# Interleaving two tensors on one core: eight equal column tiles, or tiles of 7168, 8320 and 8384 columns

## The chip, the cores and the metric

The kernel runs on one core of one Trainium2 chip. The metric is device time in microseconds for one execution, as a median over runs. The core has several compute engines, of which this kernel uses VectorE (DVE in the profile) for copies, and 16 DMA engines that move data between HBM, the chip's main memory, and SBUF, the core's working memory of 128 partitions. SyncE (SP) and ScalarE (ACT) compute nothing here; each issues transfers into a DMA queue of its own, and the same 16 DMA engines serve both queues.

## What is computed

Two float32 arrays are interleaved element by element along the last dimension.

```python
def setup_inputs():
    batch, seq, dim = 32, 256, 1024
    return {"x": randn(batch, seq, dim), "y": randn(batch, seq, dim)}   # float32

def reference(x, y):
    result = np.zeros((batch, seq, dim * 2), dtype=np.float32)
    result[..., 0::2] = x
    result[..., 1::2] = y
    return result
```

As the last dimension is doubled throughout, the arrays can be taken as flat: element i of x goes to place 2i of the output, element i of y to place 2i+1. Each input has 8,388,608 elements or 33.55 MB; 67.11 MB are read and 67.11 MB written.

## The kernel before

The flat arrays are cut into eight consecutive pieces. Piece number t starts at element `start` and holds 128 x `lw` elements, with `lw` = `WL` = 8192. A piece is read as 128 rows of `lw` consecutive elements, one row for each SBUF partition, so that neighbouring rows lie `lw` x 4 = 32,768 B apart in HBM. The output rows belonging to it are `2 * lw` elements long, 65,536 B apart.

Each piece is handled as follows.

- x and y are loaded whole into `xtile` and `ytile` (lines 58 and 59), 4 MiB each, by transfers issued from SP. Each of the two pools has two buffers, so the loads of piece t+2 wait until the copies of piece t have read the buffer.
- The piece is then worked in halves of `WS` = 4096 columns. For each half VectorE copies the x half into the even columns of `otile` (line 80) and the y half into the odd columns (line 81). `otile` has 8192 columns and two buffers, so the copy of a half waits until the store of the half before the previous one has landed.
- Each filled `otile` is stored by one transfer of 4 MiB issued from ACT (line 82). Its rows are 32,768 B long and 65,536 B apart in HBM.

The first piece differs in two points. Its x is loaded in two column halves, one issued from SP and one from ACT (line 53). After its y has landed, ACT issues a small early store (line 67), 16 rows of 128 elements from `ytile` to the place of the last piece in the output, where the last piece's own stores write the final values later.

Order around the change: SP's queue holds, in order, half of the first x, the first y, then x and y of each later piece. ACT's queue holds the other half of the first x, the early store and then the sixteen stores, numbered 1 to 16 in what follows, two for each piece. VectorE works in program order except that both x copies of the first piece run before its y copies. [...]

After the program is built, `tile_interleave_kernel` moves the first load of SP and of ACT into the opening block and shortens the closing block. The change does not touch this.

Of the kernel before, what the change touches and what calls it, by code (L numbers as in the profile page):

```python
# [3 lines left out]

# [4 lines left out]


@with_exitstack
def _interleave(
    ctx: ExitStack,
    tc: tile.TileContext,
    x: bass.AP,
    y: bass.AP,
    out: bass.AP,
):
    nc = tc.nc  # L20
    P = 128

    total = 1
    for s in x.shape:
        total *= s

    WL = 8192
    WS = 4096

    xf = x.rearrange("b s d -> (b s d)")  # L30
    yf = y.rearrange("b s d -> (b s d)")
    of = out.rearrange("b s d -> (b s d)")

    fp32 = mybir.dt.float32

    xpool = ctx.enter_context(tc.tile_pool(name="xp", bufs=2))
    ypool = ctx.enter_context(tc.tile_pool(name="yp", bufs=2))
    opool = ctx.enter_context(tc.tile_pool(name="op", bufs=2))

    lwidths = [WL] * (total // P // WL)  # L40
    assert sum(lwidths) == total // P

    start = 0
    for lw in lwidths:
        xtile = xpool.tile([P, WL], fp32, name="xtile")[:, :lw]
        ytile = ypool.tile([P, WL], fp32, name="ytile")[:, :lw]

        xs = dataclasses.replace(xf, offset=start, ap=[[lw, P], [1, lw]])
        ys = dataclasses.replace(yf, offset=start, ap=[[lw, P], [1, lw]])
        if start == 0:  # L50

            for q, c in ((nc.sync, 0), (nc.scalar, lw // 2)):
                q.dma_start(
                    out=xtile[:, c : c + lw // 2],
                    in_=dataclasses.replace(xf, offset=c, ap=[[lw, P], [1, lw // 2]]),
                )
        else:
            nc.sync.dma_start(out=xtile, in_=xs)
        nc.sync.dma_start(out=ytile, in_=ys)

        if start == 0:


            early = dataclasses.replace(
                of, offset=2 * (total - P * WL), ap=[[2 * WL, 16], [1, 128]]
            )
            nc.scalar.dma_start(out=early, in_=ytile[:16, :128])

        soff = 0
        while soff < lw:  # L70
            width = min(WS, lw - soff)
            otile = opool.tile([P, 2 * WS], fp32, name="otile")[:, : 2 * width]
            os_ = dataclasses.replace(
                of,
                offset=2 * start + 2 * soff,
                ap=[[2 * lw, P], [1, 2 * width]],
            )
            xsub = xtile[:, soff : soff + width]
            ysub = ytile[:, soff : soff + width]
            nc.vector.tensor_copy(out=otile[:, 0::2], in_=xsub)  # L80
            nc.vector.tensor_copy(out=otile[:, 1::2], in_=ysub)  # L81
            nc.scalar.dma_start(out=os_, in_=otile)
            soff += width

        start += P * lw
    assert start == total


def kernel(tc, x, y, out):
    nc = tc.nc  # L90
    _interleave(tc, x, y, out)
    tc.close()
    tc.compile()  # L93


    blocks = nc.main_func.blocks
    for engine in (mybir.EngineType.SP, mybir.EngineType.Activation):
        opening = blocks[0].instructions
        at, moved = next(
            (b, i)  # L100
            for b in blocks[1:]
            for i in b.instructions
            if i.engine == engine and i.opcode == "DMACopy"
        )
        assert not moved.sync_info.on_wait
        body = at.instructions
        body.remove(moved)
        gate = next(
            n
            for n, i in enumerate(opening)  # L110
            if i.engine == engine and i.opcode == "Drain"
        )
        opening.insert(gate, moved)
        at.instructions = body
        blocks[0].instructions = opening

    last = nc.main_func.blocks[-1]  # L120
    tail = last.instructions
    wait = tail[0]
    clear = next(n for n, i in enumerate(tail) if i.opcode == "ISA")
    assert wait.engine == mybir.EngineType.SP and wait.opcode == "Drain"
    assert wait.sync_info.on_wait and not wait.sync_info.on_update
    assert tail[clear].engine == mybir.EngineType.Pool
    last.instructions = [
        copy.replace(wait, engine=mybir.EngineType.Pool)
    ] + tail[clear:]


# [1 line left out]
_INS = ['x', 'y']  # L133
_OUTS = [((32, 256, 2048), 'float32')]


# [23 lines left out]
```

## Time and profile before

| what | value |
|---|---|
| median of 3 runs | 315.62 us (315.53 to 315.71) |
| profiled execution, its own time | 315.62 us |
| its span, first to last instruction | 313.8 us |
| bytes moved | 134.23 MB in 4784 DMA packets |
| mean rate over the span | 428 GB/s |
| share of 16 DMA engines, ACT's queue (q10) and SP's queue (q1) | 51.1% and 48.4% |
| VectorE copies, 32 of them | 2295 ns (line 80) and 2293 ns (line 81) each |
| median from issue to landing: store, y load, x load | 29.1, 60.8, 43.6 us |

The span is shorter than the time because it holds only what lies between the first and the last instruction on the core. A DMA packet here is one row going to or from one partition, or a small write that signals completion. The 128 rows of a transfer are shared out over 16 DMA engines, eight to each.

The waits of the compute engines, longest first, show what VectorE waits for: the columns are the waiting engine and line, what it waited for, the total in us, how often, and the longest.

```profile
DVE otile L80 <- DMA out_dram<-otile: 174.2, 14, 21.8
DVE otile L81 <- DMA ytile<-in_y_dram: 39.9, 8, 5.8
DVE otile L80 <- DMA xtile<-in_x_dram: 11.7, 1, 11.7
```

Line 80 waits 14 times for a store to free its `otile`; line 81 waits once in each piece for y. Both are waits for DMA transfers.

### The profile page before, as it was taken

The numbers are of one execution on the slowest core, as the hardware profiler recorded it, in microseconds if no ns is written. First come the engines' busy times: TensorE is split into PE (matmuls) and PEld (weight loads), VectorE is DVE, ScalarE is ACT, GpSimd is POOL, SyncE is SP. The second block draws the span as 40 slices with busy tenths as digits, with TensorE's granted clock in tenths as the row PEclk, the third lists the DMA queues.
The fourth block names the chain that finished last, engine by engine and source line by source line (L and its number), as shares of the span: only waits on it lengthen the run. The fifth ranks groups of instructions, "written<-read, shape, count | busy, mean of one in ns | idle before, by whom it ended". The sixth has DMA issues, their size and how long they took to land.

```text
span 313.8 us, 139 instructions
## 1 busy us (share of the span) xinstructions
DVE 72.6 (23%) x32; POOL 0.2 (0%) x4
## 2 busy tenths in 40 slices
DVE  0523002231022410325003150031501305023500
POOL 0000000000000000000000000000000000000000
DMA  8999999999999999999999999999999999999997
GB/s 340 462 405 398 459 409 459 409 459 409 459 409 447 422 439 430 426 443 422 447 414 455 409 459 401 468 401 464 405 464 405 464 405 459 409 459 409 459 409 334
DMA packets 4784, 134.23 MB, mean 428 GB/s; under 512 B 544, under 2 KB 560, under 8 KB 560
## 3 DMA queue, kind: packets, MB, share of 16 engines
q10 hardware_dynamic: 2480, 69.22, 51.1%
q1 hardware_dynamic: 2304, 65.01, 48.4%
HBM read 67.11 MB, written 67.12 MB: 428 GB/s over the span
## 4 chain that ended last, share of the span: by engine, by line
DMA 83%; DVE 11%; DVEq 1%; issue 0%
DMA out_dram<-otile 76%; DMA ytile<-in_y_dram 7%; DVE otile L81 6%; DVE otile L80 5%; DVEq L93 1%; DVEq L80 0%
## 5 line engine op out<-in xcount | busy, mean ns | idle before, releaser
L80 DVE COPY otile<-xtile 128x4096 f32<-128x4096 f32 x16 | 36.6, 2295 | 185.9 <-DMA out_dram<-otile 174.2
L81 DVE COPY otile<-ytile 128x4096 f32<-128x4096 f32 x16 | 36.6, 2293 | 39.9 <-DMA ytile<-in_y_dram 39.9
L144 POOL MEMSET const-bfloat16-1.0<- 128x1 bf16 x1 | 0.1, 101 | 0.0
L144 POOL MEMSET const-uint8-127<- 128x1 uint8 x1 | 0.1, 101 | 0.0
L144 POOL MEMSET const-float32-0.0<- 128x1 f32 x1 | 0.1, 98 | 0.2 <-issue 0.2
L144 POOL MEMSET const-float32-1.0<- 128x1 f32 x1 | 0.1, 98 | 0.0
## 6 DMA issues: line engine op xcount, KB each, us to landing
out_dram<-otile ACTq DMA_DIRECT2D x16, 4096.0 KB, 29.1
ytile<-in_y_dram SPq DMA_DIRECT2D x8, 4096.0 KB, 60.8
xtile<-in_x_dram SPq DMA_DIRECT2D x7, 4096.0 KB, 43.6
xtile<-in_x_dram SPq DMA_DIRECT2D x1, 2048.0 KB, 11.6
xtile<-in_x_dram ACTq DMA_DIRECT2D x1, 2048.0 KB, 13.3
out_dram<-ytile ACTq DMA_DIRECT2D x1, 8.0 KB, 6.2
```

The source lines that it names most:

```text
L80: nc.vector.tensor_copy(out=otile[:, 0::2], in_=xsub)
L81: nc.vector.tensor_copy(out=otile[:, 1::2], in_=ysub)
L93: tc.compile()
L144: nc = _bacc.Bacc("TRN2", target_bir_lowering=False, num_devices=1)
```

## The change

The list of widths becomes one piece of 7168 columns, five of 8320 and two of 8384, which again add up to 65,536 columns. `WL`, now 8384, is the width of the buffers and of the last piece. `WS` is set anew for each piece to half its width, so there are still two halves, two copies for each half and one store for each half: 3584, 4160 or 4192 columns to a half. The rows of the loads are now 28,672, 33,280 or 33,536 B long and as far apart; the stores' rows are as long and twice as far apart.

```diff
-    WL = 8192
-    WS = 4096
+    WL = 8384
...
-    lwidths = [WL] * (total // P // WL)
+    lwidths = [7168] + [8320] * 5 + [8384] * 2
     assert sum(lwidths) == total // P
...
             nc.scalar.dma_start(out=early, in_=ytile[:16, :128])
 
+        WS = lw // 2
         soff = 0
         while soff < lw:
             width = min(WS, lw - soff)
-            otile = opool.tile([P, 2 * WS], fp32, name="otile")[:, : 2 * width]
+            otile = opool.tile([P, WL], fp32, name="otile")[:, : 2 * width]
```

The number of loads, copies and stores, and the bytes that they move, stay the same. The early store's place in the output follows `WL`, as it is worked out from the start of the last piece.

## The prediction

> **What bounds the kernel now.** I read the page's busy shares first, then its DMA rows, then busy time by window, then the timeline and the waits. The page's engine row and its two slice rows:
>
> ```profile
> DVE 72.6 (23%) x32; POOL 0.2 (0%) x4
> ...
> DMA  8999999999999999999999999999999999999997
> GB/s 340 462 405 398 459 409 459 409 459 409 459 409 447 422 439 430 426 443 422 447 414 455 409 459 401 468 401 464 405 464 405 464 405 459 409 459 409 459 409 334
> ```
>
> VectorE is busy for a quarter of the span, the DMA engines for nine tenths or more in all slices but the first and the last. The slices swing between 401 and 468 GB/s only because a packet's bytes are counted where it starts and a slice holds a broken number of packets. Windows cut at one tile's period show no swing; the columns are window, length, VectorE busy (instructions), POOL busy, clock, DMA share, GB/s:
>
> ```profile
> 67.56:106.29 38.73, 9.09 (x4) 0.00 (x0) 1.00 1.00 433
> 106.29:145.01 38.72, 9.09 (x4) 0.00 (x0) 1.00 1.00 433
> 145.01:183.74 38.73, 9.09 (x5) 0.00 (x0) 1.00 1.00 433
> 183.74:222.46 38.72, 9.09 (x4) 0.00 (x0) 1.00 1.00 433
> 222.46:261.19 38.73, 9.09 (x5) 0.00 (x0) 1.00 1.00 433
> ```
>
> Five tiles at five different addresses take the same time to 0.01 us, 16.777 MB in 38.726 us, or 433.2 GB/s. Two more windows separate the directions, loads alone early and stores alone late:
>
> ```profile
> 11.65:22.00 10.35, 4.51 (x3) 0.00 (x0) 1.00 1.01 434
> ...
> 294.00:310.00 16.00, 4.43 (x2) 0.00 (x0) 1.00 1.01 434
> ```
>
> Loads alone, which step by 32 KiB from row to row, stores alone, which step by 64 KiB, and the mixture all run at 433 to 434. [...] The trace's packet records, which lie beneath these views, agree: of 3968 rows of 32 KiB, 3931 last exactly 1213 ns. A slow address would show as a longer row, and the longer ones but for ten are the 27 around 26 to 28 us discussed below. So the kernel is bound by the 16 DMA engines' own pace: 32 rows per engine and tile in 38.726 us, 1.2102 us for a row of 8192 columns.
>
> The time outside that pace: 134.23 MB at 433.2 is 309.85 us, and the span is 313.80, so 3.95 us lie around it. By windows, the first 2 us carry 139 GB/s and lose 1.36, the next two carry 385 and lose 0.22, the stretch from 22 to 48, where stores join the loads, carries 424 and loses 26 x (1 - 424/433.2) = 0.55, and 1.80 after 312 start no packet. Together 3.93. The profiled run took 315.62, which is 1.82 more than its span and equal to the median.
>
> **The change, part by part.** *Bytes and rows.* Eight tiles stay eight tiles, each with 32 rows per engine (8 of x, 8 of y, twice 8 of output). Scaling the row by columns, the new sum per engine is 32 x (1.0589 + 5 x 1.2291 + 2 x 1.2386) = 309.8 us, the old one 32 x 8 x 1.2102 = 309.8. A fixed cost within a row cancels too, as there are 256 rows either way. Term: 0.
>
> *The pitch.* What it can give is bounded below by nothing and above by the fastest window of some length: stores alone from 300 to 306 carry 437 GB/s, and 134.23/0.437 is 2.7 us less than 309.85; but a six-microsecond window holds five packets per engine, so that is mostly counting. In the other direction a pitch that is no power of two could stretch rows; the nearest rows for that are the ten single rows of 1216 to 1226 ns, 13 ns over the usual, and on all 256 rows of an engine that would be +3.3 us. I take 0, because the row time is the same at every address, direction and both present pitches.
>
> [...]
>
> *Copies on VectorE.* 32 copies stay 32, of 3584, 4160 and 4192 columns in place of 4096, at 2294 ns per 4096: about 2.01, 2.33 and 2.35 us. The total stays 72.6. They hide behind transfers in flight; without that cover a tile of 8384 pays 4 x 0.05 = 0.2 us more.
>
> *The start.* The first tile has 1024 columns less, so its y lands 2 x 1024 x 4 x 128 B / 433.2 = 2.42 us earlier than 21.98; its two y copies end with the first store's issue 0.28 sooner still, 24.31 becoming about 21.6. SP's later issues move with it: x of the third tile, now at 16.18, and its y, now at 28.23 behind the small early store. None of this shortens the end, because the load queue holds x and y of the second tile, issued at 1.30 and 1.94, until 55.46: the engines were busy then and still are. What is paid once when stores join, 0.55 us, could disappear or double, depending on where in a row the first store arrives. I take it unchanged; bounds -0.55 and +0.55.
>
> *The end.* The last store may not start late, so its queue must never run dry. The timeline there, with start, length, and in brackets the idle time and what ended it:
>
> ```profile
> 280.64 2.29 DVE L80 COPY otile<-xtile 128x4096 f32<-128x4096 f32 x1 [14.95 <-DMA out_dram<-otile]
> 287.81 2.29 DVE L81 COPY otile<-ytile 128x4096 f32<-128x4096 f32 x1 [4.88 <-DMA ytile<-in_y_dram]
> 290.13 8.67 ACTq L82 DMA_DIRECT2D out_dram<-otile  x2
> 293.93 2.30 DVE L80 COPY otile<-xtile 128x4096 f32<-128x4096 f32 x1 [3.83 <-DMA out_dram<-otile]
> 296.14 2.29 DVE L81 COPY otile<-ytile 128x4096 f32<-128x4096 f32 x1
> ```
>
> The last y lands at 287.81, its copy ends at 290.1, store 15 is issued, and store 14 lands at 293.84. Store 15 took 13.4 us to land, so 303.53, which is 9.69 after store 14: eight rows at 1.21, no gap. By the packet records, store 14's last rows end at 293.05 to 293.58 across engines, and the kernel's first load needed 1.0 to 2.2 us from issue to the first row on an engine. The cover is therefore 1.2 to 1.9 us. Who waits if it is gone: store 15, then the copies at 293.93 (for store 14's buffer), then store 16 behind store 15 on Activation's queue.
>
> How the cover moves depends on how many rows of store 14 are left when loads end; now it is five. The packet records show the two queues taking turns row by row, so this number is set only by how many rows of the second tile's x pass alone before the first store joins: six now, and five or six after, as the store is issued 0.28 us (a quarter of a row) sooner after y. Five left give 0.14 more cover from longer rows less 0.04 for the longer copy. Four left take off 1.24 and leave 0.1 to 0.8. I take no gap; bounds 0 and +1.5, the latter from the rival below. In the steady part the cover is larger: a first-half store is issued near 96.5 and the one before it lands at 106.2.
>
> Sum: 0 + 0 + 0 + 0 + 0; the span stays 313.8, the time 315.6.
>
> **Rivals.** *A gap before the last tile's first store* (slower). If the queues share by bytes rather than rows, the earlier start of the stores (2.42 + 0.28 = 2.7 us) pushes the loads' end back by as much; less the cover of 1.2 to 1.9 that is a gap of 0.8 to 1.5 us, about 316.8. It decides from the point where under four rows of store 14 remain when the last y lands. For it: the 3.71 us between 290.13 and 293.84 are the shortest distance in the trace. Against: the rows' strict alternation. Chance 0.14.
>
> *Rows longer than 32 KiB get cut in two, or otherwise cost a bit more each* (slower). Seven tiles have rows of 33,280 and 33,536 B. The first tile's 16 KiB rows follow one another at 607 ns, so a cut costs 2 x 607 - 1210 = 4 to 5 ns, on 28 transfers of 8 rows per engine 1.0 us: 316.6. For it: no row here is over 32,768 B. Against: nothing at that size shows a limit. Chance 0.07.
>
> *The pitch does cost today, evenly on all rows* (faster). Half of the 2.7 us bound gives 314.3. For it: a uniform loss is invisible in a comparison of rows. Against: 32 KiB loads and 64 KiB stores agree to 1 GB/s. With the switch cost of 0.55 vanishing beside a little of this, chance 0.19.
>
> **How the numbers follow.** No change beyond 0.2% (0.63 us, about what a measurement of this kernel tells from nothing) has 0.60, all of it the forecast of 315.6, whose own range is 315.1 to 316.1 from the switch bounds. Faster 0.19 and slower 0.21 are the rivals' chances. Cutting each outer tail to about one in ten, the range is 314.5 to 316.9: down to four tenths of the pitch bound, up to the gap rival's centre.
>
> **What would show it.** Right: full-width periods of 38.726 x 8320/8192 = 39.33 us at 433 GB/s, 4784 packets, the last y landing within 1.3 us of 287.8, store 15 following store 14 after 8 x 1.24 = 9.9 us. A gap: store 15 landing later than that, and a window below 400 between 288 and 296. Cut rows: more packets. A pitch effect: periods shorter than 39.2 us, over 434 GB/s. Wrong altogether would be a change of the 1.8 us at either end, where I let nothing move.

## The result, and the profile after

The changed kernel is slower: 316.59 us at the median of 16 executions (315.54 to 317.47), against 315.72 for 19 of the kernel before (315.44 to 316.57). The ratio is 1.0025, with a 95% interval of 1.0014 to 1.0036. Its executions also scatter more: its fastest, 315.54, is as fast as the old kernel, and its slowest is 1.9 us above that; the old kernel's differ by 1.1 us.

The profiled execution took 316.03 us, with a span of 314.2. Its busy shares on the page and its packet count:

```profile
DVE 72.6 (23%) x32; POOL 0.2 (0%) x4
...
DMA packets 4784, 134.23 MB, mean 427 GB/s; under 512 B 544, under 2 KB 560, under 8 KB 560
```

Copies, bytes and packets are the old ones. Windows over four tile periods in the middle, with window, length, VectorE busy, POOL busy, clock, DMA share and GB/s:

```profile
63.49:102.82 39.33, 9.22 (x4) 0.00 (x0) 1.00 1.00 433
102.82:142.22 39.40, 9.22 (x4) 0.00 (x0) 1.00 1.01 435
142.22:181.55 39.33, 9.22 (x5) 0.00 (x0) 1.00 1.00 433
181.55:220.92 39.37, 9.22 (x4) 0.00 (x0) 1.00 1.00 433
```

The pace is the forecast 39.33 us, the old one scaled by columns, with 0.07 and 0.04 us over it in two periods where the kernel before had none. The timeline of the last tile, with start, length, and in brackets the idle time and its cause:

```profile
287.63 2.35 DVE L81 COPY otile<-ytile 128x4192 f32<-128x4192 f32 x1 [4.99 <-DMA ytile<-in_y_dram]
...
293.91 2.35 DVE L80 COPY otile<-xtile 128x4192 f32<-128x4192 f32 x1 [3.94 <-DMA out_dram<-otile]
```

The last y lands at 287.63, where it was 287.81, and store 14 at 293.82, where it was 293.84. So neither the pace nor the last tile's hand-over lost anything in this execution, although its span is 0.4 us longer. The loss shows only in the records of single packets. Each of the 16 engines ends its last store with a 4-byte completion write. In the kernel before the 16 writes come at 312.51 us on the mean and 312.85 for the last engine; here at 312.56 and 313.25. The mean engine lost 0.05, the last one 0.40, and the kernel ends with the last. Most of this lag was there early. Every transfer ends with 16 such writes, one on each engine: 544 for the 34 transfers. After ACT's half of the first x, at about 12 us, the last write came 0.26 us behind the mean in the kernel before and 0.44 in this one; after store 1 it was 0.35 and 0.62, after store 16 it was 0.34 and 0.69.

A second execution of the same kernel, profiled at 318.54 us with a span of 316.7 (the run *again2* below), shows this in the windows. They count a row's bytes where the row starts. The first fence is the end of the kernel before, the second that of *again2*:

```profile
311.00:311.60 0.60, 0.00 (x0) 0.00 (x0) 1.00 1.90 819
311.60:313.80 2.20, 0.00 (x0) 0.00 (x0) 1.00 0.04 15
```

```profile
312.00:313.00 1.00, 0.00 (x0) 0.00 (x0) 1.00 1.24 537
313.00:314.00 1.00, 0.00 (x0) 0.00 (x0) 1.00 0.09 34
314.00:316.70 2.70, 0.00 (x0) 0.00 (x0) 1.00 0.03 12
```

In the kernel before, 819 GB/s over 0.6 us are 15 rows of 32,768 B, and after them one row starts: the engines finish within half a row of each other. In *again2* 537 GB/s over 1 us are 16 rows of 33,536 B, then 34 GB/s is one row, and 12 GB/s over 2.7 us is again one row. By the packet records fourteen engines end between 313.29 and 313.41, one at 314.03, and the last works alone until 315.76.

### The profile page after: what moved, and what is told of

The parts are those of the page before. It is cut to its first block, busy times and chain, and to the rows that moved or that the text cites. A ratio compares the mean times of both kernels' runs of the same rounds, so it can differ in the third digit from the quotient of the medians.

```text
span 314.2 us, 139 instructions
## 1 busy us (share of the span) xinstructions
DVE 72.6 (23%) x32; POOL 0.2 (0%) x4
## 2 busy tenths in 40 slices
DMA packets 4784, 134.23 MB, mean 427 GB/s; under 512 B 544, under 2 KB 560, under 8 KB 560
## 4 chain that ended last, share of the span: by engine, by line
DMA 83%; DVE 11%; DVEq 1%; issue 0%
DMA out_dram<-otile 77%; DMA ytile<-in_y_dram 6%; DVE otile L81 6%; DVE otile L80 5%; DVEq L93 1%; DVEq L80 0%
## 5 line engine op out<-in xcount | busy, mean ns | idle before, releaser
L80 DVE COPY otile<-xtile 128x4160 f32<-128x4160 f32 (+2 forms) x16 | 36.6, 2294 | 186.5 <-DMA out_dram<-otile 175.7
L81 DVE COPY otile<-ytile 128x4160 f32<-128x4160 f32 (+2 forms) x16 | 36.6, 2292 | 39.4 <-DMA ytile<-in_y_dram 39.4
```

## The experiments

All kernels ran beside the kernel before on the same chip. The ratios are those on record and not quotients of the two medians; that of *more_256* leaves out its slowest execution, 322.19 us. "Odd 256" counts the tiles whose rows are an odd multiple of 256 B long (8384 columns are 131 x 256 B).

```
run                first tile  odd 256  median us  before us  ratio   95% interval
result             7168        2        316.59     315.72     1.0025  1.0014 to 1.0036
again              7168        2        316.62     315.63     1.0034  1.0023 to 1.0044
again2             7168        2        316.73     315.63     1.0031  1.0022 to 1.0041
buf_8448           7168        2        316.43     315.63     1.0026  1.0016 to 1.0035
early_8448         7168        2        316.08     315.52     1.0021  1.0007 to 1.0035
more_256           7168        6        317.49     315.52     1.0054  1.0034 to 1.0074
first_narrow       7168        0        315.86     315.63     1.0011  1.0002 to 1.0019
all_512            7168        0        315.74     315.63     1.0010  0.9995 to 1.0024
all_512_b          7168        0        315.91     315.63     1.0016  1.0005 to 1.0028
narrow_last        8320        2        316.57     315.63     1.0033  1.0020 to 1.0045
wide_first         8704        0        316.11     315.63     1.0016  1.0008 to 1.0025
odd_pitch          8192        0        315.55     315.63     1.0005  0.9995 to 1.0015
before_buf_8384    8192        0        315.60     315.63     1.0000  0.9992 to 1.0009
hbm_256            8192        6        315.50     315.63     1.0001  0.9993 to 1.0010
first_8192         8192        2        315.54     315.52     1.0002  0.9993 to 1.0010
split_3584         8192        0        315.93     315.63     1.0011  1.0002 to 1.0021
before_split_4160  8192        0        315.66     315.71     0.9998  0.9989 to 1.0007
after_split_4096   7168        2        315.98     315.71     1.0005  0.9996 to 1.0014
part_7168          7168 of 8192 0       311.13     315.52     0.9867  0.9852 to 0.9882
```

**First series: start, pitch, alignment or gap.** The theories are defined in the expectations as they come up. *again* is the changed kernel without an edit.

> The changed kernel once more, as the level for the other three and for a second trace. All theories: about 316.5 us, 0.8 above the kernel before (315.7), with a scatter of some 2 us between executions. Theory START (the narrow first tile: its 14,336 B rows are read while the engines are still being set going, and an engine that loses time there ends late, since the end waits for the slowest of 16): the trace shows engines further apart after the first 8 us than the 0.8 us of the kernel before. Theory PITCH (rows at pitches of 33,280 and 33,536 B are held up now and then): the trace shows lengthened rows after 30 us, more than 0.5 us of them on the engine that ends last.

It repeated the loss. In its packet records the engine that ends last (313.85, mean 312.66) already stands 0.6 us behind the mean after 5 us: its first row took 1400 ns over the usual. It lost 0.6 more between 40 and 64 us, through four rows lengthened one at a time. Both theories find their sign here, and the next three decide.

```diff
-    lwidths = [7168] + [8320] * 5 + [8384] * 2
+    lwidths = [7168] + [8192] * 5 + [8704] * 2      # first_narrow, WL = 8704
+    lwidths = [8192] + [8320, 8064] * 3 + [8192]    # odd_pitch, WL = 8320
+    lwidths = [7168] + [8320] * 6 + [8448]          # all_512, WL = 8448
```

> Only the first tile is narrow: widths 7168, five of 8192, two of 8704, all pitches whole multiples of 2 KiB. START: as slow as the changed kernel, about 316.5. PITCH: as the kernel before, 315.7, since five tiles keep 32 KiB. Theory MISALIGN (rows of 33,536 B start at odd multiples of 256 B): 315.7. Theory GAP (the store queue runs dry before the last tile's first store): 316 to 317, with a gap visible before store 15.

> The first and the last tile have 8192 columns as before, the six between alternate 8320 and 8064, so that their rows lie 33,280 and 32,256 B apart. START: 315.7, as before. PITCH: about 316.4, nearly all of the changed kernel's loss, as six of eight tiles have such rows. MISALIGN: 315.7, since all rows are multiples of 512 B. GAP: 315.7.

> The changed kernel with its last two tiles mended to multiples of 512 B: widths 7168, six of 8320, one of 8448. START: 316.5, as the changed kernel. PITCH: 316.5 as well. MISALIGN: 315.7, as the kernel before. GAP: 316 to 317.

PITCH falls for the tiles behind the first: six of them with odd pitches cost nothing that can be measured (1.0005, 0.9995 to 1.0015), and *odd_pitch*'s trace has no lengthened row after 30 us. A narrow first tile alone, *first_narrow*, gives a third of the loss. The median of *all_512* lay where MISALIGN had put it, though its interval reaches up to 1.0024, so that theory was taken up next, split into buffers and HBM.

**Second series: which alignment.** *buf_8448* gives the changed kernel buffers of 8448 columns, *before_buf_8384* gives the old kernel buffers of 8384, and *hbm_256* has misaligned HBM rows in six tiles.

```diff
-        xtile = xpool.tile([P, WL], fp32, name="xtile")[:, :lw]
+        xtile = xpool.tile([P, 8448], fp32, name="xtile")[:, :lw]    # buf_8448, hbm_256; y and o alike; 8384 in before_buf_8384
...
+    lwidths = [8192] + [8256, 8128] * 3 + [8192]    # hbm_256, WL = 8192
```

> The changed kernel unaltered, as the level for the next three: about 316.5 us. Theory START+CHANCE (the four kernels of the first series differ only through the accidental order in which engines are set going): anything from 315.7 to 316.6, no firm level.

> The changed widths, with buffers of 8448 in place of 8384 columns, so that every buffer starts at a multiple of 512 B in a partition; HBM addresses are the changed kernel's. Theory SBUF256 (buffers at odd multiples of 256 B cost the engines): about 315.7, as all_512. Theory HBM256 (rows of the last two tiles at odd multiples of 256 B in HBM): 316.5, as the changed kernel. START+CHANCE: 315.7 to 316.6.

> The kernel before, eight tiles of 8192, but with buffers of 8384 columns, so that every second buffer starts at an odd multiple of 256 B. SBUF256: about 316.5. HBM256: 315.7. START: 315.7, since the first tile is the old one.

> Buffers of 8448 columns; widths 8192, three times 8256 and 8128 in turn, 8192, so that the rows of six tiles lie at odd multiples of 256 B in HBM. HBM256: three times the changed kernel's two such tiles, 317 to 318. SBUF256: 315.7. START: 315.7, since the first tile is the old one.

Both forms fall as causes by themselves. The buffers' place changes nothing in either direction (316.43 and 315.60), and six tiles of odd rows after an old first tile stand at 315.50. *again2* holds the slowest execution of its ten and shows what an engine out of step does. The first row of its last engine took 1786 ns too long; by 120 us that engine was 1.3 us behind the mean, by 240 us 2.2. The last tile on its timeline:

```profile
290.13 2.35 DVE L81 COPY otile<-ytile 128x4192 f32<-128x4192 f32 x1 [5.21 <-DMA ytile<-in_y_dram]
...
296.39 2.35 DVE L80 COPY otile<-xtile 128x4192 f32<-128x4192 f32 x1 [3.91 <-DMA out_dram<-otile]
```

The last y lands at 290.13, 2.5 us later than in the other trace of this kernel. The first copy of y waits for all 16 engines: in all eight tiles of the two profiled kernels, before and changed, it starts 0.37 to 0.40 us after the last of the load's 16 completion writes, which are spread over 0.5 to 1.0 us. By the packet records nearly all other engines then had to wait 0.7 to 0.9 us for store 15. The gap forecast as a rival does occur, but as a consequence of one late engine, which ends later still.

**Third series: narrow, wide, or merely not 8192.**

```diff
+    lwidths = [8320] * 5 + [8384] * 2 + [7168]          # narrow_last
+    lwidths = [8704] + [8064] * 4 + [8192] * 3          # wide_first, WL = 8704
...
-            for q, c in ((nc.sync, 0), (nc.scalar, lw // 2)):
+            for q, c, w in ((nc.sync, 0, 3584), (nc.scalar, 3584, 4608)):    # split_3584, in the kernel before
```

In the first two, and in the other kernels whose last tile is not `WL` wide, the early store keeps its place at the last tile's output.

> Widths 7168, six of 8320, one of 8448 once more: was its 315.74 a property of the widths or chance? Theory START (a narrow first tile sets the 16 engines going unevenly): about 316.3 and long rows after 30 us in the trace. Theory LAST (two last tiles of 8384 are needed as well): 315.7 again.

> The changed kernel's widths with the narrow tile moved to the end: five of 8320, two of 8384, 7168 last. START as narrowness: 315.6, engines no further apart after 5 us than in the kernel before (at most 2.3 us of lag), no long rows after 30 us. START as any first pitch but 32 KiB: 316.5. LAST: 316.5.

> First tile of 8704 columns, rows 34 KiB apart, then four of 8064 and three of 8192. START as narrowness: 315.6. START as any first pitch but 32 KiB: 316.3 or more, with long rows in the trace.

> The kernel before, eight tiles of 8192, with the first x cut into 3584 and 4608 columns in place of halves: the first rows on SP's queue are 14,336 B long as in the changed kernel, but 32 KiB apart. START by the length of the first rows: 316.3 or more, with long rows. START by their pitch: 315.6, no long rows.

Narrowness falls: with the narrow tile moved to the end and a first tile of 8320 columns the loss is all there (1.0033, five executions), and a wider first tile costs half of it, without the long rows that its theory had asked for. *all_512_b* lies between its two theories: its widths lose less than the changed kernel's, but this time something (1.0016). *split_3584* lies between its theories too: cutting the old first x unevenly costs 0.3 us on the median, so a first tile of 8192 columns alone is no guarantee.

**Fourth series: the first tile alone undone.**

```diff
+    lwidths = [8192] + [8320] * 5 + [7872] * 2              # first_8192
+    lwidths = [7168] + [8384] * 4 + [8256] * 2 + [8320]     # more_256
...
-                of, offset=2 * (total - P * WL), ap=[[2 * WL, 16], [1, 128]]
+                of, offset=2 * (total - P * 8448), ap=[[2 * 8448, 16], [1, 128]]    # early_8448
...
+            lw = 7168                                       # part_7168, kernel before, first tile; row pitch stays 8192
```

> The change with its first tile alone undone: widths 8192, five of 8320, two of 7872 (rows of 31,488 B, odd multiples of 256 B). Theory START (first rows 32 KiB apart set the 16 engines going evenly, others don't): 315.6, longest first-row delay under 1.0 us, no long rows after 30 us. Theory LAST (the two last tiles at odd multiples of 256 B, whatever the first): 316.3 or more.

> Narrow first tile as in the change, then six tiles at odd multiples of 256 B in place of two: 7168, four of 8384, two of 8256, 8320. START alone: 316 to 316.6. LAST, or START and LAST together: 317 or more, since three times as many tiles carry it.

> The changed kernel, with only its small early store moved to where the widths 7168, six of 8320 and 8448 have it (16 rows, 67,584 B apart, in place of 67,072). Theory EARLY (the place of this first write decides how unevenly the engines take up the stores): 315.8. START, LAST: 316.5 as the changed kernel.

> The kernel before, whose first tile handles only columns 0 to 7167 of its 8192 (the other 1024 columns of that tile are left out of the output), with rows still 32 KiB apart: the change's first rows in length and time, the old pitch. Work less by 2.097 MB, or 4.84 us: 310.8 if only the bytes count. START by pitch: 310.8, longest first-row delay under 1.0 us. START by narrowness or by the earlier stores: 311.2 to 311.8, with long rows as in the changed kernel.

*first_8192* settles the place. With the first tile back at 8192, the five odd-pitch tiles kept and two misaligned ones still at the end, the whole loss is gone (1.0002, 0.9993 to 1.0010). The last two tiles had to give up the columns that the first one regained, 7872 in place of 8384 each, so they changed too. The end of its windows reads as that of the kernel before, 14 to 15 rows and then one alone (its rows have 31,488 B):

```profile
311.00:311.60 0.60, 0.00 (x0) 0.00 (x0) 1.00 1.82 787
311.60:313.70 2.10, 0.00 (x0) 0.00 (x0) 1.00 0.04 15
```

*more_256* suggests that tiles at odd multiples of 256 B deepen the loss if the first tile is not 8192: with 7168 first in two equal halves, none of them gives 1.0010 to 1.0016, two 1.0021 to 1.0034, six 1.0054; with 8192 first, two and six give 1.0002 and 1.0001. Only six against none stands clear of the intervals (1.0034 and up against 1.0028 at most), and the other widths differ between these kernels as well. *early_8448* lies between its two theories and decides nothing by itself; but *wide_first* has the early store where the kernel before has it and still loses, so its place cannot be the whole cause. *part_7168* ran only four times (310.79 to 312.28). Against the 310.7 that the bytes leave of 315.52 its median is 0.45 too high (by the interval of its ratio, 0.2 to 1.1), and its trace has the lengthened rows; the old pitch with shorter rows is thus no cure, which speaks against the first tile's pitch as the property that counts.

**Fifth series: the very first rows.** The first x is cut at column 4096 of 7168 in the changed kernel, and at 4160 of 8192 in the kernel before, by the edit shown for *split_3584*.

> The changed kernel with the first x cut into 4096 and 3072 columns in place of 3584 and 3584: SP's first rows are 16,384 B long as in the kernel before, 28 KiB apart. Theory START by row length (first rows of 16,384 B set the engines going evenly): 315.6 to 315.8, longest first-row delay under 1.0 us. START by the width of the whole first tile: 316.5 as the changed kernel, delay over 1.05 us.

> The kernel before with its first x cut into 4160 and 4032 columns, rows of 16,640 and 16,128 B in place of 16,384 twice, and nothing else changed. START by row length: 315.9 or more, delay over 1.05 us, as with 3584 and 4608 columns (315.93). START by the width of the whole first tile, or by an uneven cut: 315.6, delay under 1.0 us.

Neither theory holds whole. First rows of 16,384 B bring the changed kernel down to 315.98, most of the way, though its interval still holds 0.14% and its trace has one row held for 617 ns. First rows of 16,640 B cost the old kernel nothing. The longest first-row delay was 1.09 us in the first trace and 1.10 in the second, so that sign fails as well: 1.10 went with no loss. That the length of the very first rows is all that matters is refuted.

The packet records behind this, for the trace of each run. "At first x" and "at end" tell how far the last engine's completion write came behind the mean of the 16, after ACT's half of the first x (at 11 to 14 us) and after store 16; "long rows" counts rows over 20 ns too long after 30 us, up to the last load. All times are in us.

```
trace              at first x  mean end  last end  at end  long rows  time of that execution
before                0.26      312.51    312.85    0.34       0        315.62
before_buf_8384       0.29      312.53    312.81    0.28       0        315.60
odd_pitch             0.20      312.36    312.59    0.23       0        315.35
hbm_256               0.28      312.43    312.64    0.21       0        315.41
first_8192            0.27      312.51    312.77    0.26       0        315.54
before_split_4160     0.28      312.60    312.87    0.27       0        315.63
split_3584            0.30      312.42    312.62    0.20       1        315.41
early_8448            0.32      312.44    312.69    0.26       0        315.48
wide_first            0.41      312.71    313.08    0.37       0        315.87
all_512               0.53      312.55    313.08    0.53       9        315.87
after                 0.44      312.56    313.25    0.69       1        316.03
first_narrow          0.50      312.48    313.30    0.82       7        316.08
buf_8448              0.50      312.78    313.35    0.57       0        316.12
narrow_last           0.61      312.90    313.59    0.69      12        316.37
more_256              0.61      312.59    313.74    1.15      11        316.54
again                 0.55      312.66    313.85    1.19       4        316.62
after_split_4096      0.51      312.54    313.93    1.39       3        316.71
all_512_b             0.80      312.96    314.01    1.05      15        316.78
again2                0.95      313.54    315.76    2.23      26        318.54
part_7168             0.54      307.73    309.50    1.76      12        312.28
```

In all twenty the execution's time is 2.76 to 2.80 us more than the last engine's completion write, so the time follows the last engine. In the upper eight that engine is at most 0.32 us behind at the first x and 0.34 at the end; in the other twelve it is 0.41 or more behind at the first x already, and 0.37 to 2.2 at the end. The kernels of *early_8448* and *split_3584* lose on the median and were caught here in even executions. The lag is not all of the loss: the mean engine too ends 0.2 to 0.5 us later than in the kernel before in *wide_first*, *buf_8448*, *narrow_last* and *all_512_b*, and 1.0 later in *again2*, where the others had waited for the late one.

## Why the prediction was wrong

Most of its steps held. The pitch of the tiles behind the first gives nothing and takes nothing (*odd_pitch* 1.0005, *hbm_256* 1.0001, *first_8192* 1.0002), so the faster rival falls. Bytes and rows: 4784 packets, none cut, periods of 39.33 to 39.40 us against 39.33; the rival of cut rows falls. The copies stay hidden, 9.22 us of VectorE in a period of 39.33. The end: the last y within 0.2 us of its old place, and store 15, which took 13.7 us, lands 9.9 us after store 14, so there is no gap; in *again2* a gap appears, with another origin than the one named. That 316.59 lies inside the stated range, at the place of the two slower rivals (316.8 and 316.6), is luck: neither of their mechanisms made the loss.

The step that failed is *The start*: "I take it unchanged; bounds -0.55 and +0.55", on the ground that "the engines were busy then and still are". For the 16 engines' mean in the profiled execution that came out: the mean end moved by 0.05 us. The term that the prediction bounded did not move either: rows that began between 20 and 32 us, where the stores join, ran 0.72 us over their usual length per engine in both traces. But the sum treated the 16 engines as one server whose terms cancel. They are 16 servers with fixed shares: in six of the traces the rows can be followed from end to start on every engine, and each handles 264. What the last one had lost stayed lost (0.35 us behind the mean after store 1 and 0.34 after store 16 in the kernel before, 0.62 and 0.69 in the changed one), and in all twenty traces the execution's time is 2.76 to 2.80 us more than that engine's last write.

What the sum lacks is the last engine's lag behind the mean: its change was put at nothing, and no reason given. The lag measured 0.34 us before, and 0.69 in the profiled execution of the changed kernel, which lost 0.41 us in all. In *again*, whose profiled execution stands at the changed kernel's median loss, the lag was 1.19 and the mean end 0.15 later, which makes up its 1.0 us. The records held such a lag before the change: the engines' last rows of store 14 were quoted as ending between 293.05 and 293.58 (the records have 292.95 to 293.49, about the same width). That spread is itself a term of the time, and the change of the first tile enlarges it: with that tile undone, and the last two adjusted, the whole 0.9 us is gone. The forecast's last sentence, that it would be wrong altogether by a change at either end of the span, comes near it: the lag begins at the first rows and shows at the end, although the time after the last write stayed as it was.

What is shown is the place (the first tile) and the form (single engines behind, by their first rows, by about 13 us, and by rows held later). That tiles at odd multiples of 256 B add to it is likely (1.0054 with six of them behind a first tile of 7168 columns, 1.0010 to 1.0016 with none). What stays open is why a first tile of 8192 columns in two equal halves sets the engines going evenly and most others tried do not: neither pitch, narrowness nor the length of the very first rows explains all runs. Whether one cause makes both the uneven starts and the rows held later is open as well: *buf_8448* and *wide_first* started unevenly and lost time without a row held after 30 us. No version that writes the whole output beat the kernel before beyond its interval; the lowest medians, 315.50 to 315.55, are its equals.

## What to carry to other kernels

Here the DMA share was 1.00 to 1.01 in all windows of a tile, and equal bytes went with nearly the same end of the mean engine, 312.51 and 312.56 us in the profiled executions; but the time was the last engine's, 2.76 to 2.80 us after its last write. So in such a kernel look at how far apart the engines finish, and how far apart they were after the first transfers. An edit of no cost to the sum widened that spread here, from 0.34 to 0.69 us between the last engine and the mean, so compare scatter between executions as well as medians. Undo an edit part by part before believing the reason it was made for: here the later tiles' pitch was neutral, and the first tile, which took the columns that were left, carried the loss.

## What the runs showed of the hardware

- Rows of a load or store took a time linear in their length with a small constant, about 8 ns by these values: 535 ns for 14,336 B, 611 for 16,384, 1062 for 28,672, 1213 for 32,768, 1232 for 33,280, 1241 for 33,536 (the commonest value of each), at all pitches tried and in both directions.
- The first row on an engine took longer than that by 0.3 to 0.8 us in the trace of the kernel before, by 0 to 1.09 in that of the changed kernel and by up to 1.79 in *again2*, differently on each engine. Once the stores had joined, the last engine's lag stayed where no row was held: in the kernel before it was 0.34 or 0.35 us after each of the 16 stores. In the changed kernel it was 0.62 us after stores 1 to 5, then a row at 122 us was held for 82 ns, and it was 0.69 or 0.70 from store 6 on.
- In all twenty traces the time is 2.76 to 2.80 us more than the last engine's last completion write, wherever the mean engine ends.
- Rows an odd multiple of 256 B long, so that every second one starts at such a place, cost nothing measurable behind an even start (1.0001, 0.9993 to 1.0010, with six of eight tiles), yet went with 1.0054 (1.0034 to 1.0074) where the engines started unevenly.
